# Strassen's scheme for the down projections of both MLPs, with spilled operand quarters

## The chip, the cores and the metric

The kernel runs on one core of one Trainium2 chip. The metric is the device time in microseconds (us) of one execution. TensorE (PE in the profile) multiplies matrices, VectorE (DVE) and ScalarE (ACT) work elementwise and read PSUM, GpSimd (POOL) works elementwise in SBUF, and all DMAs of this kernel are issued from SyncE's queue (SP).

## What is computed

Two layers over 1024 prompt tokens and 32 sample tokens, of width 1024. Layer 0 has a Mamba-2 mixer, layer 1 stick-breaking attention. After each mixer stands the same MLP, and it is all that matters here:

```python
def sq_relu_mlp(h, w_up, w_down):
    return jnp.square(jax.nn.relu(h @ w_up)) @ w_down

y_p = y_p + sq_relu_mlp(rms_norm(y_p, norm_mlp[i]), mlp_up[i], mlp_down[i])
y_s = y_s + sq_relu_mlp(rms_norm(y_s, norm_mlp[i]), mlp_up[i], mlp_down[i])
```

`w_up` is 1024 x 4096 and `w_down` 4096 x 1024, all in float32.

## The kernel before

Both token groups are one activation matrix X of T = 1056 columns (tokens), kept transposed as 8 tiles of 128 rows (features). A float32 product is made of three matmuls: each operand is split into a high part (rounded, type fp32r) and a low part (the rest), and high x high, high x low and low x high are accumulated in PSUM. A split is one copy on ACT (the high part) and one subtraction on DVE (the low part).

The MLP runs twice, as "a" after the Mamba mixer and "b" after attention (`mlp`, L918 to L975); "b" is the end of the kernel.

**Up projection** (class `Up`, L646). The hidden layer has 32 tiles f of 128 rows. Tiles 0 and 1 are made plainly (`plain`, L728). The other 30 are made in 15 pairs by Strassen's scheme (Winograd's form): `pair` (L807) takes two output tiles (f and g), four blocks k of the 1024 inputs, each split in two, and two halves of the tokens (HW = 528 columns each). In place of 8 block products there are 7, of 4 x 3 x 2 = 24 matmuls each, 264 columns wide (`product`, L795, matmuls at L803). The sums of operands on the side of X are made once (`mix12`, `mix4`, `mix3`); those on the side of the weights are made for each pair by `wprep` (L753), whose seven pieces (load, two pieces of sums on POOL and DVE, four splits) are placed as side work between the products of the pair before. The products' results are combined on DVE (L841 to L860), squared on ACT (L834), and spilled to DRAM: tensor `v_d` holds 32 tiles of 128 x 1056, stored in halves at L835. Four PSUM buffers of two banks each rotate.

**Down projection** (L967 to L974). It is plain. In 8 blocks b of four f-tiles each, `mids` (L904) loads the four spilled tiles (L899) and splits them (ACT L900, DVE L901); `down_block` (L625) then goes through the 8 output tiles d, four f-tiles x 3 terms x 3 column groups of 352 (GW) for each, 36 matmuls at L145, and `accum` (L612) adds the PSUM result to X[d] on DVE (L620). Weights come two output tiles at a time (512 KB) through `load_w` (L115: load L117, splits L123 and L124). So a down projection is 8 x 8 x 36 = 2304 matmuls. The X tiles were parked in DRAM (`x_s`) while the up projection used their place, and `reload` (L958) brings them back around the last pair.

The last block of "a" calls `done(d)` after each output tile: X[d] is stored and enters the norm of the attention layer (splits at L185 and L186), and the first projection of attention (L1433) follows. The last block of "b" goes group by group (`gstep`, L164) and stores the output (L1442 to L1446).

**What sets the order.** The program lists the work of all engines in one order; the framework's scheduler then gives each engine its queue, in which an instruction may stand earlier than in the program if its data and buffers are free by then. On the chip each queue runs in order, and an instruction that waits holds up those behind it. SBUF tiles with the same tag share a buffer: a new tile waits until the old one's readers are done.

Of the kernel before, what the change touches and what calls it, by code (L numbers as in the profile page):

```python
# [20 lines left out]
NG = 3  # L21
# [25 lines left out]
NC_COLS = C_HALF + 4  # L47

# [29 lines left out]
def hybrid_step(ctx: ExitStack, tc: tile.TileContext, xt, cst, cbf, w_in, w_dt, w_out, w_up0, w_dn0, w_qkv, w_o,  # L78
# [23 lines left out]
    xg = [None] * KD  # L102

# [23 lines left out]
    def gemm(src, xs, pp, evac, name, f0=0, w=None, tag="g", gmajor=False, mid=None, step=4,  # L127
             grp=GRP):

        box = {}  # L130
        nk = len(xs)

# [4 lines left out]
        def kstep(k):  # L137
            if k == 0:
                start()
# [3 lines left out]
            for i, (a, b) in enumerate(((wh, xh), (wh, xl), (wl, xh))):  # L143
                for g in range(NG):
                    te.matmul(box["ps"][g][:, :GW], a[:, c:c + 128], b[:, GRP[g]],  # L145
                              start=(k == 0 and i == 0), stop=(k == nk - 1 and i == 2))
            if k == nk - 1:
# [23 lines left out]
        return [lambda k=k: kstep(k) for k in range(nk)]  # L171
# [474 lines left out]
    class Up:  # L646
# [5 lines left out]
        def __init__(self, mp, name, gain_col, w, order):  # L652
            self.mp, self.name, self.gain, self.w, self.order = mp, name, gain_col, w, order
            self.v_d = dp.tile([32, 128, T], F32, name=f"v_d{name}", tag=f"v_d{name}")
# [3 lines left out]
            self.prepared = {}  # L658

# [93 lines left out]
        def wprep(self, p):  # L753
# [18 lines left out]
            def sums2():  # L772
# [3 lines left out]
                gp.tensor_tensor(S4, part(r0, 1), part(S, 0), op=ALU.subtract)  # L776

            def split(key):
                raw = w[key]
                if key == "S4":  # L780
                    hi, lo = (self.mp.tile([128, 512], F32R, name=f"w{n}3_{nm}", tag=f"w{n}4", bufs=1) for n in "hl")
                    sc.activation(hi, raw, AF.Copy)
                    ve.tensor_tensor(lo, raw, hi.bitcast(F32), op=ALU.subtract)
                else:
                    hi, lo = split_w(raw, f"{nm}_{key}")
# [8 lines left out]

        def product(self, ps, p, j, ks, first):  # L795

            (wh, wl), c0 = self.prepared[p][j]
            for k in ks:
                c = c0 + 128 * k
                xh, xl = self.ops[j, k]  # L800
                for i, (a, b) in enumerate(((wh, xh), (wh, xl), (wl, xh))):
                    for g in range(2):
                        te.matmul(ps[:, g, :QW], a[:, c:c + 128], b[:, QW * g:QW * g + QW],  # L803
                                  start=(first and k == 0 and i == 0), stop=(k == 3 and i == 2),
                                  skip_group_check=not first)

        def pair(self, p, side):  # L807
# [15 lines left out]
            def two(t):  # L823
                return t[:, :, :QW]

            def sp(x):
                return x.rearrange("p (g n) -> p g n", g=2)

            def out(n, h, e):
# [5 lines left out]
                dma(self.v_d[2 * p + (n == "g")][:, HW * h:HW * h + HW], c)  # L835
# [38 lines left out]
            then()  # L874
            self.product(A, p, 2, K, False)
# [4 lines left out]
            then()  # L880
            B = psum()
            self.product(B, p, 3, K, True)
            p7(B)
            p5(C)
            then()
# [5 lines left out]
            p3(C)  # L891
            while side:
# [11 lines left out]
        def mids(self, b):  # L904

            xs = []
            kind = "xl" if b == 6 else "m" if b % 2 == 0 or b == 7 else "xh"
            for i in range(4):
                h, l = (f"{kind}{2 * i + n}" for n in range(2))
                xs.append(self.parts(self.v_d[4 * b + i], (h, l), f"m{self.name}{b}{i}"))  # L910
            return xs

        def project(self, tail):

            for p in range(1, 16):
                self.pair(p, self.wprep(p + 1) if p < 15 else [lambda: None] * 3 + tail)

    def mlp(X, src, w_last, gain_col, w_up, w_dn, mp, pp, close_pp, stp, name, order, last=None, each=None):  # L918
# [9 lines left out]
        prep = up.wprep(1)  # L928
# [622 lines left out]
```

## Time and profile before

| | us |
|---|---|
| median of 3 runs | 3080.03 (3076.19 to 3080.2) |
| profiled execution | 3083.55 |
| its span, first to last instruction | 3081.8 |
| up projection a, pairs 1 to 15, from | 998.73 |
| down projection a, from | 1305.61 |
| projection that follows, from | 1674.95 |
| up projection b, pairs 1 to 15, from | 2401.25 |
| down projection b, from | 2709.01 |

The starts are those of the chain of work that ended last. The granted TensorE clock is 0.993 over the span. In the profile, `ps_ua` and `ps_da` are the PSUM tiles of the up and the down projection of "a", `ps_ub` and `ps_db` those of "b"; `y_ma`, `yh_ma` and `yo_ma` are a spilled tile, its high and its low part; `ws`, `wh` and `wl` are weights, raw, high and low. A row of a group reads: line, engine, operation, output <- inputs, shapes, count | busy us, mean ns of one | idle us of the engine before them, and what ended it.

### The profile page before, as it was taken

How to read it: one execution, taken by the hardware profiler on the slowest of the kernel's cores; microseconds unless marked ns; L12 is line 12 of the kernel's file. 1: busy time of each engine (PE TensorE's matmuls, PEld its weight loads, DVE VectorE, ACT ScalarE, POOL GpSimd, SP SyncE). 2: the span in 40 equal slices, each digit the busy share in tenths (PEclk: the TensorE clock that was granted, in tenths of full speed). 3: DMA queues.
4: the chain of work that ended last, by engine and by line, in shares of the span. 5: the costliest groups of instructions: out<-in, count | busy, mean ns of one | idle time of the engine just before them, and what ended most of it. 6: DMA issues, size and time to landing. Idle time of an engine off the chain costs nothing.

```text
span 3081.8 us, 52128 instructions
## 1 busy us (share of the span) xinstructions
PE 3020.6 (98%) x21438; PEld 2881.1 (93%) x21438; DVE 1963.1 (64%) x2858; ACT 1168.0 (38%) x1959; POOL 750.0 (24%) x591
## 2 busy tenths in 40 slices
PE   9999999999999999999999999999999999999999
PEld 7899888898999999999999888888889999999999
DVE  7877788776748655644534677677668755554443
ACT  4433333334224333311203466666664433321210
POOL 2666656665100111000002133233230111100000
PEclk9999999999999999999999999999999999999999
DMA  4323333333522433543312322222234323352311
GB/s 134 72 74 79 71 78 84 78 83 93 185 90 92 136 112 102 168 132 105 117 44 85 113 78 71 70 70 71 84 108 141 122 99 112 128 183 84 119 62 71
DMA packets 142631, 308.01 MB, mean 100 GB/s; under 512 B 18380, under 2 KB 67768, under 8 KB 142392
## 3 DMA queue, kind: packets, MB, share of 16 engines
q1 hardware_dynamic: 142392, 304.67, 32.4%
q8 instruction: 169, 2.77, 0.4%
q14 instruction: 70, 0.57, 0.1%
HBM read 220.25 MB, written 75.98 MB: 96 GB/s over the span
## 4 chain that ended last, share of the span: by engine, by line
PE 80%; DVE 13%; issue 3%; ACT 2%; DMA 2%; POOL 1%; SPq 0%; DVEq 0%; ACTq 0%; POOLq 0%
PE ps_da L145 12%; PE ps_db L145 10%; PE ps_ua L803 9%; PE ps_ub L803 9%; PE ps_i L164 9%; PE ps_q L164 3%; PE ps_o L164 3%; PE ps_k L164 2%; PE o L1234 2%; PE wt L1218 2%; PE ps_v L164 2%; PE ps_o L145 2%; PE ps_lb L145 1%; PE ps_db L164 1%; PE ps_la L145 1%
## 5 line engine op out<-in xcount | busy, mean ns | idle before, releaser
L164 PE MATMUL ps_i<-xh_n,wh_i 128*128 128x352 f32 x1056 | 359.3, 340 | 0.0
L164 PE MATMUL ps_i<-xh_n,wl_i 128*128 128x352 f32 x1056 | 343.8, 326 | 0.0
L164 PE MATMUL ps_i<-xl_n,wh_i 128*128 128x352 f32 x1056 | 343.7, 325 | 0.0
L1183 POOL TENSOR_TENSOR b<-b,p 128x255 f32<-128x255 f32 (+7 forms) x128 | 165.3, 1292 | 378.6 <-DVE p L1181 236.4
L1181 DVE TENSOR_TENSOR_SCAN p<-p 128x255 f32<-128x255 f32 (+7 forms) x128 | 192.2, 1502 | 91.7 <-ACT p L1179 90.6
L164 PEld LDWEIGHTS ps_i<-xh_n,wh_i 128*128 128x128 f32 x1056 | 201.8, 191 | 13.5 <-issue 11.6
L620 DVE TENSOR_TENSOR X_b<-X_b,ps_db 128x352 f32<-128x352 f32 x192 | 89.9, 517 | 180.9 <-PE ps_db L145 150.5
L164 PEld LDWEIGHTS ps_i<-xl_n,wh_i 128*128 128x128 f32 x1056 | 203.0, 192 | 0.0
L164 PEld LDWEIGHTS ps_i<-xh_n,wl_i 128*128 128x128 f32 x1056 | 201.3, 191 | 0.0
L620 DVE TENSOR_TENSOR X_a<-X_a,ps_da 128x352 f32<-128x352 f32 x192 | 88.5, 516 | 168.9 <-PE ps_da L145 168.9
L145 PE MATMUL ps_da<-yh_ma,wl_da 128*128 128x352 f32 x768 | 164.8, 323 | 0.0
L145 PE MATMUL ps_da<-yh_ma,wh_da 128*128 128x352 f32 x768 | 164.7, 323 | 0.0
L145 PE MATMUL ps_da<-yo_ma,wh_da 128*128 128x352 f32 x768 | 164.7, 323 | 0.0
L448 ACT ACTIVATE L<-L,naT 128x128 f32<-128x128 f32 (+1 forms) x288 | 89.7, 382 | 166.9 <-POOL L L445 166.9
L145 PE MATMUL ps_db<-yh_mb,wl_db 128*128 128x352 f32 x672 | 144.2, 323 | 0.0
L145 PE MATMUL ps_db<-yh_mb,wh_db 128*128 128x352 f32 x672 | 144.1, 323 | 0.0
L145 PE MATMUL ps_db<-yo_mb,wh_db 128*128 128x352 f32 x672 | 144.1, 323 | 0.0
L145 PEld LDWEIGHTS ps_da<-yh_ma,wl_da 128*128 128x128 f32 x768 | 130.4, 188 | 0.0
L145 PEld LDWEIGHTS ps_da<-yh_ma,wh_da 128*128 128x128 f32 x768 | 130.3, 188 | 0.0
L145 PEld LDWEIGHTS ps_da<-yo_ma,wh_da 128*128 128x128 f32 x768 | 130.3, 188 | 0.0
L1179 ACT ACTIVATE p<-z,qn_q 128x384 f32<-128x384 f32 (+4 forms) x192 | 104.5, 579 | 60.2 <-PE z L1210 29.4
L124 POOL TENSOR_TENSOR wl_i<-ws_i,wh_i 128x1024 fp32r<-128x1024 f32 x44 | 106.5, 2420 | 70.4 <-ACT wh_i L123 70.3
(764 smaller groups left out, 8419.4 us busy)
## 6 DMA issues: line engine op xcount, KB each, us to landing
ws_i<-in_w_in SPq DMA_DIRECT2D x48, 512.0 KB
y_ma<-v_da SPq DMA_DIRECT2D x32, 528.0 KB
y_mb<-v_db SPq DMA_DIRECT2D x32, 528.0 KB
ab<-acs_d SPq DMA_DIRECT2D x64, 256.0 KB
ws_da<-in_w_dn SPq DMA_DIRECT2D x32, 512.0 KB
ws_db<-in_w_dn SPq DMA_DIRECT2D x32, 512.0 KB
ws_a<-in_w_up SPq DMA_DIRECT2D x30, 512.0 KB
ws_b<-in_w_up SPq DMA_DIRECT2D x30, 512.0 KB
```

The lines of the kernel that those rows point to most:

```text
L124: eng[0].tensor_tensor(lo, st, hi.bitcast(F32), op=ALU.subtract)
L145: te.matmul(box["ps"][g][:, :GW], a[:, c:c + 128], b[:, GRP[g]], start=(k == 0 and i == 0), stop=(k == nk - 1 and i == 2))
L164: te.matmul(box["ps"][:, :n], a[:, c:c + 128], b[:, grp[g]], start=(k == 0 and i == 0), stop=(k == nk - 1 and i == 2))
L448: sc.activation(L[0:w, h, :w], L[0:w, h, :w], AF.Exp, bias=naT[0:w, c, 4 * g + h:4 * g + h + 1])
L620: ve.tensor_tensor(X[d][:, GRP[g]], X[d][:, GRP[g]], ps, op=ALU.add)
L803: te.matmul(ps[:, g, :QW], a[:, c:c + 128], b[:, QW * g:QW * g + QW], start=(first and k == 0 and i == 0), stop=(k == 3 and i == 2), skip_ ...
L1179: sc.activation(t[0:np_, c:c + w], ps[0:np_, :w], AF.Sigmoid, scale=sn[0:np_, f])
L1181: ve.tensor_tensor_scan(p[0:np_, 1:W][:, ::-1], p[0:np_, 1:W][:, ::-1], p[0:np_, 1:W][:, ::-1], 1.0, op0=ALU.mult, op1=ALU.bypass)
L1183: gp.tensor_tensor(b[0:np_, 0:W - 1], b[0:np_, 0:W - 1], p[0:np_, 1:W], op=ALU.mult)
L1218: te.transpose(ps[:, c, :], self.b[:, 128 * (c0 + c):128 * (c0 + c) + 128], ident)
L1234: te.matmul(o[r, :128], V[:, c, r], u.wt[c // 4 * 4][:, c % 4, :], start=(c == 0), stop=(c == i))
```

## The change

The down projection uses the same seven-product scheme, for both MLPs. Its 2 x 2 blocks are: two output tiles d (a "pair", four of them), the two f-tiles of one f-pair k (16 of them), and two halves of the tokens.

- Up projection: for each f-pair, `mix` makes four sums of the halves of f and g on DVE, and seven quarters of 128 x 528 (the operands of the seven products) are spilled to `q_d` in place of four to `v_d`. The second half of f is no longer spilled itself. f-pair 0 (from `plain`) is mixed during pair 1. In pair 15, product 3 is moved ahead.
- Down projection: 19 steps in place of 8 blocks. Four f-pairs are resident, as seven split operands each, in the tiles that held the operands of the up projection. A step takes one output pair and all resident f-pairs that it lacks (`STEPS`: two, three and four at the start, mostly four, then three, two and one at the end), and sums them in PSUM. While a step runs, `refill` loads, splits and so replaces one f-pair (7 quarters), each operand right after the product that used it last; `wprep`, now with n f-pairs wide, makes the next step's weights (`w_dn` is laid out anew on the host).
- PSUM: three accumulators U, W, V of two banks in a step, and a fourth buffer from which the next step's U starts. Seven additions of 528 columns to X per step, on DVE; U is read out after each of its four products and then added onto further.
- X tiles return in another order of tags; `done` and the output's stores follow the order in which output pairs end (6, 7, then 0, 1, then 2, 3, then 4, 5), and the next projection takes its inputs in that order (`ks`).

The core of the diff:

```diff
+QPOS = (4, 1, 3, 5, 0, 2, 6)
+ORDER = (0, 2, 1, 4, 3, 6, 5)
+
+STEPS = [(s % 4, ks) for s, ks in enumerate(
+    [range(0, 2), range(0, 3), range(0, 4), range(0, 4), range(2, 5), range(3, 6), range(4, 7)] +
+    [range(max(s - 3, 4), min(s + 1, 16)) for s in range(7, 19)])]
...
+        def mix(self, k, f, g, ta, tb):
+
+            (f0, f1), (g0, g1), (t1, t2), (t3, t4) = ([x[:, HW * h:HW * h + HW] for h in range(2)] for x in (f, g, ta, tb))
+            ve.tensor_tensor(t1, f1, f0, op=ALU.subtract)
+            ve.tensor_tensor(t2, g1, t1, op=ALU.subtract)
+            self.spill(k, 4, ta)
+            ve.tensor_tensor(t3, g1, f1, op=ALU.subtract)
+            ve.tensor_tensor(t4, g0, t2, op=ALU.subtract)
+            self.spill(k, 3, tb)
...
             self.product(C, p, 6, K, False)
             p3(C)
+            self.mix(p, *(box[n] for n in ("f", "g", "t1", "t2")))
...
+        def refill(self, k):
+
+            box = {}
+
+            def f(j):
+                n = ORDER.index(j)
+                if n % 2 == 0:
+                    box["y"] = self.mp.tile([128, T], F32, name=f"y_{self.name}{k}{j}", bufs=2 if n < 4 else 1,
+                                            tag=("sq", "sq", "acc", "u0")[n // 2])
+                    for i, jj in enumerate(ORDER[n:n + 2]):
+                        dma(box["y"][:, HW * i:HW * i + HW], self.q_d[k, QPOS.index(jj)])
+                t = self.ttile(DTAGS[k % 4][n], f"d{j}_{self.name}{k}")
+                self.split(j, ("d", k), box["y"][:, HW * (n % 2):HW * (n % 2) + HW], t[:, 0:HW], t[:, HW:T])
+
+            return [lambda j=j: f(j) for j in ORDER]
...
+        def step(self, s, X, side, each):
...
+            ps = {n: self.psum.tile([128, 2, 512], F32, name=f"ps_d{self.name}{s}{n}", tag=f"d{r[n]}") for n in "UWV"}
+            self.roles = {"U": r["F"], "V": r["W"], "W": r["V"], "F": r["U"]}
+            K = [("d", k) for k in ks]
+            for n, (j, c, first, d, h, end) in enumerate((
+                    (0, "U", True, d1, 0, False), (2, "W", True, d1, 0, True), (1, "U", False, d1, 1, False),
+                    (4, "V", True, d2, 1, False), (3, "U", False, d2, 1, True), (6, "V", False, d1, 1, True),
+                    (5, "U", False, d2, 0, True))):
+                self.product(ps[c], f"d{s}", j, K, first)
+                x = self.sp(X[d][:, HW * h:HW * h + HW])
+                ve.tensor_tensor(x, x, self.two(ps[c]), op=ALU.add)
+                if end:
+                    each(d, h)
+                for t in side:
+                    if n < len(t) and t[n]:
+                        t[n]()
...
-            self.pair(p, self.wprep(p + 1) if p < 15 else [lambda: None] * 3 + tail)
+                prep = self.up_weights(p + 1) if p < 15 else tail
...
-            up.project([lambda: box.update(xs=up.mids(0)), first, lambda: reload((0, 1, 3, 5))])
-        reload((2, 4, 6, 7))
+            up.project([lambda: (dw[0](), reload((0, 1))), dw[1], lambda: (run(r0[:3]), dw[2]()),
+                        lambda: (run(r0[3:6]), dw[3]()), lambda: (run(r0[6:] + r1[:3]), dw[4]()),
+                        lambda: (run(r1[3:5]), dw[5](), reload((2, 3))), lambda: (dw[6](), run(r1[5:]))])
+        reload(range(4, KD))
...
-        for b in range(8):
-            end = b == 7
-            blk = down_block(w_dn[b], box["xs"], X, pp, f"d{name}{b}", done if end else None, gmajor=bool(each) and end,
-                             each=each if end else None, first=box.pop("w", None))
+        refills = {0: r2, 1: up.refill(3), **{s: up.refill(k) for s, k in ((3, 4), (4, 5), (5, 6), (6, 7))},
+                   **{s: up.refill(s + 1) for s in range(7, 15)}}
...
+            for s, (pair, _) in enumerate(STEPS):
...
+                side = [refills.get(s, [])]
+                if s + 1 < len(STEPS):
+                    side.append(up.down_weights(s + 1))
+                up.step(s, X, side, finished)
```

More of the change, by code (lines that the diff above doesn't have):

```diff
@@ L102, in hybrid_step @@
     xg = [None] * KD
+    xtags = [(f"xh{d}", f"xl{d}") for d in range(KD)]
     rota = {"ws": [0, 1], "wh": [0, 1, 2], "wl": [0, 1, 2]}
@@ L803, in product, with two, sp @@
                         te.matmul(ps[:, g, :QW], a[:, c:c + 128], b[:, QW * g:QW * g + QW],
-                                  start=(first and k == 0 and i == 0), stop=(k == 3 and i == 2),
+                                  start=(first and n == 0 and i == 0), stop=(n == len(ks) - 1 and i == 2),
                                   skip_group_check=not first)
+        def two(self, t):
+            return t[:, :, :QW]
+        def sp(self, x):
+            return x.rearrange("p (g n) -> p g n", g=2)
         def pair(self, p, side):
@@ L874, in pair @@
             then()
+            if p == 15:
+                B = psum()
+                self.product(B, p, 3, K, True)
+                p7(B)
+                then()
             self.product(A, p, 2, K, False)
@@ L879, in pair @@
             self.product(C, p, 4, K, True)
[L880 to L885, printed above, removed]
+            if p == 15:
+                p5(C)
+                then()
+            else:
+                then()
+                B = psum()
+                self.product(B, p, 3, K, True)
+                p7(B)
+                p5(C)
+                then()
             B = psum()
@@ L950, in mlp, with reload @@
         close_pp()
+        up.w_dn = w_dn
+        hold = [f"h{order[d]}" for d in (0, 1, 3, 5, 2, 4, 6, 7)]
+        r0, r1, r2 = (up.refill(k) for k in range(3))
+        dw = up.down_weights(0)
+        def reload(ds):
+            for d in ds:
+                X[d] = hx.tile([128, T], F32, name=f"X_{name}{d}", tag=hold[d])
+                dma(X[d], up.x_s[d])
         with ExitStack() as pu:
             up.psum = pu.enter_context(tc.tile_pool(name=f"pu{name}", bufs=4, space=PSUM, reuse_waits="tile"))
-            box = {}
@@ new lines, in mlp, with finished @@
+        reload(range(4, KD))
+        done = last(mp) if last else None
+        final = {pair: s for s, (pair, _) in enumerate(STEPS)}
+        refills = {0: r2, 1: up.refill(3), **{s: up.refill(k) for s, k in ((3, 4), (4, 5), (5, 6), (6, 7))},
+                   **{s: up.refill(s + 1) for s in range(7, 15)}}
+        with ExitStack() as pd:
+            up.psum = pd.enter_context(tc.tile_pool(name=f"pd{name}", bufs=1, space=PSUM, reuse_waits="tile"))
+            up.roles = {"U": 0, "V": 2, "W": 3, "F": 1}
+            for s, (pair, _) in enumerate(STEPS):
+                ended = []
+                def finished(d, h):
+                    if final[d // 2] != s:
+                        return
+                    if each:
+                        each(d, h)
+                    ended.append(d)
+                    if done and ended.count(d) == 2:
+                        done(d)
+                side = [refills.get(s, [])]
+                if s + 1 < len(STEPS):
+                    side.append(up.down_weights(s + 1))
+                up.step(s, X, side, finished)
```

116 lines of the change are left out of this document (65 added, 51 removed).

## The prediction

> **What bounds the kernel now.** I read the page's busy table first, then the chain in order of time, then the busy table by stage, then the groups of the engines that the change loads.
>
> ```profile
> span 3081.8 us, 52128 instructions
> PE 3020.6 (98%) x21438; PEld 2881.1 (93%) x21438; DVE 1963.1 (64%) x2858; ACT 1168.0 (38%) x1959; POOL 750.0 (24%) x591
> PE 80%; DVE 13%; issue 3%; ACT 2%; DMA 2%; POOL 1%; SPq 0%; DVEq 0%; ACTq 0%; POOLq 0%
> ```
>
> TensorE (PE) carries 80% of the chain that ended last. The next rows are pieces of that chain (start, length, what):
>
> ```profile
> 998.73 289.13 PE ps_ua L803 x2382
> 1292.08 6.50 DMA y_ma<-v_da
> 1302.45 3.16 PE ps_ua L803 x24
> 1305.61 369.34 PE ps_da L145 x2304
> 1674.95 11.62 PE ps_k L145 x72
> 2401.25 285.40 PE ps_ub L803 x2352
> 2709.01 323.22 PE ps_db L145 x2016
> 3032.23 46.09 PE ps_db L164 x288
> ```
>
> The down projection of the first MLP is one unbroken run of 2304 matmuls, 352 columns wide: 369.34/2304 = 160.3 ns each. The second takes 323.22 + 46.09 = 369.31 us. The up projection, already in Strassen's form, uses 264 columns: 289.13/2382 = 121.4 and 285.40/2352 = 121.3 ns; I use 121.35. So time per matmul follows the columns almost exactly (121.35/160.3 = 0.757, 264/352 = 0.75). One piece on the chain is no matmul: a DMA at 1292, between up and down. By stage (us, then busy time of PE, its weight loads, DVE, ACT, POOL; granted clock, DMA share, GB/s):
>
> ```profile
> 998.70:1284.00 285.30, 285.30 (x2353) 285.30 (x2352) 170.50 (x223) 97.57 (x132) 40.57 (x28) 1.00 0.34 113
> 1284.00:1305.60 21.60, 20.80 (x171) 20.59 (x170) 13.99 (x17) 10.68 (x13) 0.00 (x0) 1.00 0.86 291
> 1305.60:1328.00 22.40, 22.40 (x142) 22.40 (x141) 12.11 (x18) 6.61 (x8) 0.00 (x0) 1.00 0.88 307
> 1328.00:1674.90 346.90, 346.90 (x2166) 346.90 (x2165) 156.04 (x242) 72.92 (x68) 15.13 (x6) 1.00 0.28 90
> 1301.50:1320.00 18.50, 17.70 (x117) 17.55 (x116) 11.42 (x16) 7.26 (x9) 0.00 (x0) 1.00 0.96 341
> PE ps_ua L803 <- DVE g_a L851: 0.8, 1, 0.8
> PE ps_ub L803 <- DVE g_b L851: 1.7, 1, 1.7
> ```
>
> Both projections keep PE full at granted clock 1.00 with VectorE (DVE) at 60% and 45%. The seam between them is different: DMA at 0.86 to 0.96 of its engines, 341 GB/s at best, and PE waits 0.8 us there in the first MLP, 1.7 us in the second (last two rows).
>
> **The matmuls (the gain).** New count per MLP: 4 output pairs x 16 f-pairs x 7 products x 3 (high/low terms) x 2 column groups = 2688, all 264 wide, same operand forms as the up projection. 2688 x 0.12135 = 326.2 us against 369.3: 43.1 us less per MLP, 86.3 us for both (738.65 - 652.4).
>
> [...]
>
> **DVE in a step of the new loop.** The rows that price it:
>
> ```profile
> L859 DVE TENSOR_TENSOR f_b<-ps_ub,t_b 128x528 f32<-128x528 f32 x14 | 9.9, 707 | 2.1 <-PE ps_ub L803 2.1
> L699 DVE TENSOR_TENSOR xl_ub<-u_b,xh_ub 128x528 fp32r<-128x528 f32 x4 | 2.6, 706 | 0.0
> L783 DVE TENSOR_TENSOR wl_b<-wS_b,wh_b 128x512 fp32r<-128x512 f32 x15 | 10.2, 682 | 0.0
> L124 DVE TENSOR_TENSOR wl_da<-ws_da,wh_da 128x1024 fp32r<-128x1024 f32 x32 | 39.0, 1219 | 0.2 <-ACT wh_da L123 0.2
> L770 DVE TENSOR_TENSOR ws_b<-ws_b 128x512 f32<-128x512 f32 x14 | 9.7, 693 | 34.2 <-POOL wS_b L769 34.2
> L123 ACT ACTIVATE wh_da<-ws_da 128x1024 fp32r<-128x1024 f32 x32 | 33.9, 1059 | 204.5 <-PE ps_da L145 193.5 <-DVE yo_ma L901 6.6 <-PE ps_ua L803 2.3
> L834 ACT ACTIVATE g_a<-g_a x28: 625/628/648, 1017.8 to 1284.6; 128x528 f32<-128x528 f32 x28
> L769 POOL TENSOR_TENSOR wS_a<-ws_a,ws_a x14: 1287/1295/4735, 1006.7 to 1266.8; 128x512 f32<-128x512 f32 x14
> ```
>
> A step that takes four f-pairs: 168 matmuls, 20.4 us of PE. DVE: 7 additions from PSUM into X at 0.707 (4.9), 7 low parts of refilled operands at 0.706 (4.9), weights 3 x 1.219 + 0.682 + 2 x 0.693 = 5.7; together 15.5 us. ScalarE (ACT): 7 x 0.628 + 3 x 1.059 + 0.6 = 8.2. POOL: 2 x 1.295 = 2.6. All under 20.4, so hidden. A step of three (steps 1, 4, 5, 6, 16; 15.3 us of PE): weights shrink to three quarters, about 4.4, so 14.2 us, and 15.5 where the step after it takes four. That is 93 to 101% of PE's time, on a queue that runs in order: I take 1 us of PE waiting per MLP, bounds 0 (instructions start 0.62 us apart back to back, rows below) and 5 (1 us in each). The additions have cover: U is added to X after each of its four products, and PE writes U again only one product later, 2.9 us in a step of four, against 0.7 us of addition. If the DVE queue ran later than that, PE would wait for all that exceeds it.
>
> In the up projection each pair gains 4 subtractions (4 x 0.706 = 2.8 us of DVE) and 3 quarters more of spill. DVE goes from 170.50/285.30 = 60% to about 74%, DMA from 113 GB/s to some 153 (0.81 MB more per 20.4 us). The subtractions stand behind the pair's last read of PSUM, and the next one is due two products (5.8 us) later: that hides them, and I cost them at nothing; without that cover a pair would lose at most these 2.8 us.
>
> **The seam.** Most of the loss should lie here. Rows for it:
>
> ```profile
> 1280.90 0.70 DVE L833 SCALAR_TENSOR_TENSOR g_a<-g_a,rstd 128x528 f32<-128x528 f32 x1
> 1281.52 0.70 DVE L855 TENSOR_TENSOR g_a<-ps_ua,t_a 128x528 f32<-128x528 f32 x1
> 1282.21 1.23 DVE L124 TENSOR_TENSOR wl_a_raw<-ws_a,wh_a_raw 128x1024 fp32r<-128x1024 f32 x1
> 1283.35 0.70 DVE L833 SCALAR_TENSOR_TENSOR g_a<-g_a,rstd 128x528 f32<-128x528 f32 x1
> 1010.75 1.58 SPq L899 DMA_DIRECT2D y_ma<-v_da  x2
> 1290.32 2.08 SPq L899 DMA_DIRECT2D y_ma<-v_da  x2
> v_da<-f_a SPq DMA_DIRECT2D x30, 264.0 KB
> y_ma<-v_da SPq DMA_DIRECT2D x32, 528.0 KB
> ws_da<-in_w_dn SPq DMA_DIRECT2D x32, 512.0 KB
> ```
>
> Back to back, a 528-wide instruction starts 0.62 us after the one before, a 1024-wide one takes 1.14. The program places the loads of the first spilled tiles in the last pair, but the first two left at 1010.75, as soon as data and buffers were there; so the loads of f-pair 0 (four free buffers) will be early too. The rest is not. DMA: from about 16 us before the end of pair 15 to the start of step 2 (16 + 25.5 us; steps 0 and 1 are 84 + 126 matmuls), the queue moves 11 quarters of spill and 21 of refill for f-pairs 1 to 3 (32 x 0.27 MB), eight X tiles (8 x 0.54) and the weights of steps 1 and 2 (0.79 + 1.05): 14.8 MB. At 341 GB/s that is 43.4 us against 41.5. DVE: between the end of pair 15 and step 2, some 32 instructions of 528 (2 for the last quarter of pair 15, 4 mixing, 14 additions, 12 low parts) at 0.63 are 20.2 us, the weights of step 1 about 4.0 and the first half of step 2's 3.5: 27.7 us against 25.5. Both are 2 us over. As a refill load must wait for the split that frees its buffer, they don't overlap perfectly: I take 5 us per MLP, bounds 0 and 15 (one third of the 43.4). PE's present 0.8 + 1.7 us fall into these, so the seams cost 2 x 5 - 2.5 = 7.5 net.
>
> **The ends.**
>
> ```profile
> 3078.35 0.52 DVE L620 TENSOR_TENSOR X_b<-X_b,ps_db 128x352 f32<-128x352 f32 x1 [1.40 <-PE ps_db L164]
> L186 DVE SCALAR_TENSOR_TENSOR xl_n<-X_a,cs,xh_n 128x1056 fp32r<-128x1056 f32 x7 | 9.2, 1319 | 5.3 <-ACT xh_n L185 5.0
> ```
>
> The last step takes one f-pair: 42 matmuls, 0.73 us a product. The addition (0.707) no longer hides behind one product, and seven of them in a row need 7 x 0.707 = 4.9 of its 5.1 us, with a turn between PE and DVE at each write of U: 1 us of waiting, and 0.2 for a wider last addition (0.707 for 0.52). In the second MLP I take 1.5. In the first, two low parts of the norm (1.319 each) stand in the same DVE queue, and the next projection wants the PSUM banks of U: 2.5. It starts with d = 6 and 7, done four steps before, and reaches d = 4 and 5 six eighths of 11.62 us later, so those splits are hidden. Together 4, bounds 1 and 8.
>
> **Sum.** Span 3081.8 and the profiled execution's 3083.55 us; the median of the runs is 3080.03, 3.5 lower. 3083.55 - 86.3 + 2 x 1 + 7.5 + 4 = 3010.75; less 3.5: 3007 us.
>
> **Rivals.**
> (1) The seam is worse: SP's queue, in order, holds refill and weight loads behind X tiles that wait for pair 15's spills. For: the DMA on the chain at 1292. Against: X from f-pair 2 on is wanted only 25 us later. At the upper bound, 15 us a seam, it gives 3007 + 20 = 3027.
> (2) DVE's in-order queue becomes the bound in every step, and the kernel is slower. Each of the 11 low parts per step stands behind a copy on ACT, which stands behind a load; while DVE waits, additions behind it wait, and PE for them. The present loop does show such waits:
>
> ```profile
> L901 DVE TENSOR_TENSOR yo_ma<-y_ma,yh_ma 128x1056 fp32r<-128x1056 f32 x32 | 40.2, 1258 | 33.2 <-ACT yh_ma L900 33.1
> ```
>
> 33.2/32 = 1.04 us before each. With a wait w, the 14 steps with refills take 213 + 154w us (9 + 4 of them at 15.5 or 14.2 plus 11w, step 0 likewise), the others 73: equal to 369.3 at w = 0.54, where this decides. At 1.04 the loop takes 446 us, 76.5 more per MLP: 3080 + 153 = 3233. Against: DVE had nothing else queued in those waits, and before the weights' low parts, which have the same shape of dependency, the wait is 0.2 us over 32 (the L124 row).
> (3) A matmul costs the same at 264 as at 352 columns, as it would if weight loads set the pace: 2688 x 160.3 ns = 430.9 us, 61.6 more per MLP, 3203. Against: the 121.35 ns of the up projection, which loads as many weights per matmul. [...]
>
> **How the numbers follow.** Measurement tells about 0.2% (6 us) from no change. Chances: the forecast 0.75 (2992 to 3022), (1) 0.15, (2) 0.06 (of it 0.02 near w = 0.54, within 0.2%), (3) 0.01, and 0.03 for a result below 2992, since nothing in the sum gains beyond the matmuls. Faster 0.93, same 0.02, slower 0.05. Range: all unknown costs at their lower bounds give 3080 - 86.3 - 2.5 + 1 = 2992; at their upper, 3080 - 86.3 - 2.5 + 30 + 10 + 8 = 3039.
>
> **What would show it.** Right: the down groups count 2688 matmuls each at the up projection's 283 ns duration, in a run of 326 to 330 us; PE waits for DVE or DMA gather in the 45 us around the seam and the last 10 us of each down loop; DVE 75% busy between. Wrong: waits of PE on the additions to X spread over all steps (2); one gap of 10 us or more after pair 15 with DMA at 0.9 (1); a mean spacing well above 121 ns without waits (3).

## The result, and the profile after

| | before | after |
|---|---|---|
| median of 4 runs, us | 3078.21 (3076.19 to 3080.2) | 3095.03 (3091.33 to 3097.83) |
| profiled span, us | 3081.8 | 3096.1 |
| mean granted TensorE clock | 0.993 | 0.987 |

After/before is 1.0054 (95% interval 1.0037 to 1.0071): slower by 0.5%, where 3007 us was forecast. The forecast was wrong by 88 us, and in sign. The page of the profile after, its span, busy table and chain:

```profile
span 3096.1 us, 55134 instructions
PE 2962.8 (96%) x22206; PEld 2809.7 (91%) x22206; DVE 2272.8 (73%) x3192; ACT 1292.1 (42%) x2207; POOL 851.6 (28%) x667
PE 64%; DVE 20%; DMA 5%; issue 5%; ACT 3%; POOL 2%; SPq 0%; DVEq 0%; POOLq 0%; ACTq 0%
```

PE has less work, as forecast, but only 64% of the chain is PE now (80% before): DVE, DMA and issue have taken its place. The busy table by stage, first for most of up projection "a", then for steps 4 to 14 of its down projection (columns as in the prediction):

```profile
1000.00:1285.00 285.00, 281.98 (x2322) 281.56 (x2321) 213.41 (x274) 95.89 (x130) 42.23 (x28) 1.00 0.45 154
1399.00:1629.70 230.70, 214.47 (x1725) 211.66 (x1724) 165.92 (x217) 84.17 (x118) 30.56 (x22) 0.99 0.42 129
```

In the up projection the load is as forecast (DVE 75%, 154 GB/s) and PE misses 3 us. In the down projection PE idles 16.2 of 230.7 us, although no other engine is near full (DVE 72%): that is waiting, not work. The waits of PE and of DVE in steps 7 to 13 of "a" (engine, line, waited for: us in total, times, longest):

```profile
PE ps_da8U L857 <- DVE X_a L1018: 2.1, 1, 2.1
PE ps_da12U L857 <- DVE X_a L1018: 1.9, 1, 1.9
PE ps_da10U L857 <- DVE X_a L1018: 1.8, 1, 1.8
...
DVE ws_ad L819 <- POOL wS_ad L818: 20.1, 7, 3.3
DVE d_a L719 <- ACT d_a L718: 9.4, 15, 0.7
```

Each step has one wait of PE for an addition to X (L1018), and one wait of DVE, 20.1/7 = 2.9 us, in a sum of weights (L819) for POOL's sum (L818). How the two hang together is seen in step 8, on SP, POOL, DVE and PE (start, length, engine, line; at the end, the idle time before it and what ended it):

```profile
1473.78 0.55 SPq L810 DMA_DIRECT2D ws_ad<-in_w_dn  x1
...
1478.62 1.29 POOL L818 TENSOR_TENSOR wS_ad<-ws_ad,ws_ad 128x512 f32<-128x512 f32 x1 [17.81 <-DMA ws_ad<-in_w_dn]
1481.99 1.61 POOL L825 TENSOR_TENSOR wS_ad<-ws_ad,wS_ad 128x512 f32<-128x512 f32 x1 [2.08 <-DVE wS_ad L823]
...
1479.93 0.69 DVE L819 TENSOR_TENSOR ws_ad<-ws_ad 128x512 f32<-128x512 f32 x1 [3.27 <-POOL wS_ad L818]
1480.54 0.69 DVE L1018 TENSOR_TENSOR X_a<-X_a,ps_da8W 128x528 f32<-128x528 f32 x1
1481.16 0.68 DVE L823 TENSOR_TENSOR wS_ad<-ws_ad,ws_ad 128x512 f32<-128x512 f32 x1
1481.76 0.70 DVE L719 TENSOR_TENSOR d_a<-y_a,d_a 128x528 fp32r<-128x528 f32 x1
1482.38 2.30 DVE L836 TENSOR_TENSOR wl_ad_raw<-ws_ad,wh_ad_raw 128x1024 fp32r<-128x1024 f32 x1
1484.61 0.69 DVE L1018 TENSOR_TENSOR X_a<-X_a,ps_da8U 128x528 f32<-128x528 f32 x1
...
1485.35 0.75 PE L857 MATMUL ps_da8U<-d_a,wh_ad_S 128*128 128x264 f32 x4 [2.09 <-DVE X_a L1018]
```

Read it from the top. There are two buffers for raw weights. The second load for step 9 leaves SP at 1473.78, when the split that reads that buffer is over; POOL subtracts when it has landed (1478.62); DVE's sum waits 3.27 us for POOL and holds up what is queued behind it: the addition of W, three more operations, and the addition of U at 1484.61, for which PE stands still 2.09 us. One of the operations between, the low part of a weight, took 2.30 us where the same form takes 1.23 elsewhere; POOL works beside it from 1481.99.

The seam shows something else. The same table, before in the first row, after in the others:

```profile
1310.00:1325.00 15.00, 15.00 (x95) 15.00 (x95) 7.71 (x13) 3.77 (x4) 0.00 (x0) 1.00 0.94 321
```

```profile
1315.00:1320.00 5.00, 3.08 (x24) 2.87 (x24) 4.58 (x8) 1.93 (x3) 0.00 (x0) 1.00 0.89 287
1320.00:1325.00 5.00, 1.84 (x6) 1.53 (x7) 2.38 (x5) 0.84 (x1) 1.03 (x2) 0.52 0.95 343
1325.00:1330.00 5.00, 5.00 (x24) 5.00 (x24) 3.36 (x4) 1.13 (x2) 0.97 (x1) 0.50 0.91 325
1330.00:1335.00 5.00, 5.00 (x42) 5.00 (x41) 3.47 (x5) 3.46 (x6) 0.00 (x0) 0.96 1.04 388
```

PE stood still for 3.88 us from 1318.1, for a weight of step 1:

```profile
1321.95 1.25 PE L857 MATMUL ps_da1U<-d_a,wh_ad_raw 128*128 128x264 f32 x4 [3.88 <-ACT wh_ad_raw L835]
```

The granted clock fell to 0.50 in the course of this wait: from 1325 to 1330 PE was busy throughout and made 24 matmuls where 42 fit. In the clock record of this trace the fall stands at 1320.2, 2.1 us into the wait, and the clock stayed at half for 10.2 us. PE was busy for 7.3 of these, which at half the clock lost 3.6 us: so that wait was paid nearly twice. In that time PE had one more gap, of 1.21 us; whether this delayed the return isn't shown.

### The profile page after: what moved, and what is told of

Same layout as the page of the kernel before. It is cut to its first block, busy times and chain, and to the rows that moved or that the text cites. A ratio compares the mean times of both kernels' runs of the same rounds, so it can differ in the third digit from the quotient of the medians.

```text
span 3096.1 us, 55134 instructions
## 1 busy us (share of the span) xinstructions
PE 2962.8 (96%) x22206; PEld 2809.7 (91%) x22206; DVE 2272.8 (73%) x3192; ACT 1292.1 (42%) x2207; POOL 851.6 (28%) x667
## 4 chain that ended last, share of the span: by engine, by line
PE 64%; DVE 20%; DMA 5%; issue 5%; ACT 3%; POOL 2%; SPq 0%; DVEq 0%; POOLq 0%; ACTq 0%
PE ps_i L181 9%; PE ps_ub L857 9%; PE ps_ua L857 8%; PE ps_q L181 3%; PE ps_o L181 3%; PE ps_k L181 2%; PE o L1356 2%; PE wt L1340 2%; PE ps_v L181 2%; PE ps_o L162 2%; PE ps_lb L162 1%; PE ps_p L181 1%; DVE p L1303 1%; DMA ws_ad<-in_w_dn 1%; PE ps_la L162 1%
## 5 line engine op out<-in xcount | busy, mean ns | idle before, releaser
L818 POOL TENSOR_TENSOR wS_a<-ws_a,ws_a 128x512 f32<-128x512 f32 x15 | 24.9, 1661 | 387.0 <-DMA ws_a<-in_w_up 372.8
L140 POOL TENSOR_TENSOR wl_i<-ws_i,wh_i 128x1024 fp32r<-128x1024 f32 x44 | 105.4, 2395 | 73.7 <-ACT wh_i L139 73.5
L463 POOL TENSOR_TENSOR L<-ab,cs 128x512 f32<-128x512 f32 (+1 forms) x72 | 103.1, 1433 | 52.9 <-PE pb L498 43.4
L718 ACT ACTIVATE d_b<-y_b 128x528 fp32r<-128x528 f32 x112 | 70.8, 640 | 110.6 <-DMA y_b<-q_db 16.5
L718 ACT ACTIVATE d_a<-y_a 128x528 fp32r<-128x528 f32 x112 | 70.7, 640 | 107.1 <-DMA y_a<-q_da 13.8
L1340 PE MATMUL wt<-cs,b 128*128 128x128 f32 x576 | 90.4, 281 | 14.8 <-DVE wts L1345 12.3
L1301 ACT ACTIVATE b<-z,qn_q 128x384 f32<-128x384 f32 (+4 forms) x192 | 104.3, 584 | 0.0
L818 POOL TENSOR_TENSOR wS_bd<-ws_bd,ws_bd 128x512 f32<-128x512 f32 (+3 forms) x19 | 21.9, 1153 | 296.4 <-DMA ws_bd<-in_w_dn 272.1
L818 POOL TENSOR_TENSOR wS_b<-ws_b,ws_b 128x512 f32<-128x512 f32 x15 | 24.0, 1600 | 284.6 <-DMA ws_b<-in_w_up 254.6
L818 POOL TENSOR_TENSOR wS_ad<-ws_ad,ws_ad 128x512 f32<-128x512 f32 (+3 forms) x19 | 23.3, 1225 | 275.6 <-DMA ws_ad<-in_w_dn 255.8
L719 DVE TENSOR_TENSOR d_b<-y_b,d_b 128x528 fp32r<-128x528 f32 x112 | 82.0, 742 | 21.6 <-ACT d_b L718 20.9
L719 DVE TENSOR_TENSOR d_a<-y_a,d_a 128x528 fp32r<-128x528 f32 x112 | 81.0, 735 | 18.4 <-ACT d_a L718 17.5
```

The lines of the kernel that those rows point to most:

```text
L140: eng[0].tensor_tensor(lo, st, hi.bitcast(F32), op=ALU.subtract)
L463: gp.tensor_tensor(L[0:w, :, :w], ab[0:w, :, :w], cs[0:w, None, C_MASK:C_MASK + w].to_broadcast([w, 4, w]), op=ALU.add)
L718: sc.activation(hi, x, AF.Copy)
L719: ve.tensor_tensor(lo, x, hi.bitcast(F32), op=ALU.subtract)
L818: gp.tensor_tensor(part(S, 1), part(r0, 0), part(r1, 0), op=ALU.subtract)
L1301: sc.activation(t[0:np_, c:c + w], ps[0:np_, :w], AF.Sigmoid, scale=sn[0:np_, f])
```

## Where the time went

A step's length is taken from its first matmul on U to that of the next; "over" is what goes beyond 121.35 ns per matmul (66.3 us for steps 0 to 3, 244.6 for 4 to 16, 15.3 for 17 and 18, in each MLP). Both MLPs together, against the profiled execution before; the two columns on the right are the second and the twelfth experiment below:

| us | forecast | after | sums behind additions | all once more |
|---|---|---|---|---|
| matmuls | -86.3 | -86.3 | -86.3 | -86.3 |
| all ahead of the first down loop | 0 | +5.1 | +8.1 | +6.3 |
| steps 0 to 3, over | +10 | +37.4 | +20.6 | +12.6 |
| steps 4 to 16, over | +2 | +43.5 | +3.0 | +1.3 |
| steps 17 and 18, over (less 3.5 at the end of before) | +4 | +15.3 | +16.2 | +10.1 |
| from the first down loop to the second | 0 | -0.7 | -1.4 | +7.2 |
| sum (the forecast less 2.5 for waits of before) | -73 | +14 | -40 | -49 |

The spans differ by +14.3, -39.8 and -48.9.

## The experiments

Theory A: DVE's in-order queue. A sum of weights that waits for a late load stands ahead of additions to X that are due, and PE waits for those. Rival B: POOL's sums beside them stretch DVE's operations with two SBUF inputs (2.30 us for 1.23 in step 8), and PE waits for that. Rival C: the bytes at the seam.

Each measurement below is the median of four runs in us, then its ratio to the kernel before, run beside it, with the 95% interval.

**1. A third buffer for raw weights.** The down loop's raw weights rotate over three tiles (the third is one that lies idle there), so that a load needn't wait for the last split.

```diff
-                    w[f"raw{i}"] = wtile("ws", F32, f"{nm}_{i}")
+                    slot = raws.pop(0) if raws else None
+                    if slot is not None:
+                        raws.append(slot)
+                    w[f"raw{i}"] = (wtile("ws", F32, f"{nm}_{i}") if slot is None else rstd[:, 0:1024] if slot == 2 else
+                                    wp.tile([128, 1024], F32, name=f"ws_{nm}_{i}", tag=f"ws{slot}"))
```

> Edit: in the down loop the raw weights rotate over three buffers (the two of before and the idle tile rstd), so the loads for the next step no longer wait for the last split of this one. Theory A (the additions to X stand in VectorE's in-order queue behind a weight sum that waits for a late load; PE waits 1.7 us for them in each step of four): the wait of VectorE for POOL before L819 goes, steps 7 to 14 take 20.5 to 21 us in place of 22.4, the kernel gains 20 to 30 us (about 3068). Rival B (VectorE is short of time because POOL's two sums block its instructions with two SBUF inputs): POOL works as much as before, steps stay at 22 us, 3090 to 3095.

Measured: 3050.58 us, 0.9907 (0.9892 to 0.9922). Steps 7 to 15 took 20.4 us each in both MLPs (22.0 to 24.2 for 7 to 14 after the change). In step 7 of this run:

```profile
1462.55 0.69 DVE L823 TENSOR_TENSOR ws_ad<-ws_ad 128x512 f32<-128x512 f32 x1 [1.19 <-POOL wS_ad L822]
1463.16 0.70 DVE L1023 TENSOR_TENSOR X_a<-X_a,ps_da7V 128x528 f32<-128x528 f32 x1
...
1466.22 1.98 DVE L840 TENSOR_TENSOR wl_ad_raw<-rstd,wh_ad_raw 128x1024 fp32r<-128x1024 f32 x1
```

(Edits shift the line numbers of some runs: L823 and L840 here are L819 and L836 above.) With the load no longer late the sum waits 1.19 us, less than POOL's own 1.29, and PE no longer waits in these steps. The stretched operation is still there (1.98 us): a stretch of that size alone didn't make PE wait here.

**2. The weight sums behind the additions.** Only the order on DVE: both sums are placed after the third product, and side work is issued behind the addition of the same product.

```diff
-                ve.tensor_tensor(x, x, self.two(ps[c]), op=ALU.add)
+                added = ve.tensor_tensor(x, x, self.two(ps[c]), op=ALU.add)
...
-                        t[n]()
+                        with tc.issue_after(added.ins):
+                            t[n]()
...
-                    side.append(up.down_weights(s + 1))
+                    load, s1, s2, *rest = up.down_weights(s + 1)
+                    side.append([load, None, lambda s1=s1, s2=s2: (s1(), s2()), *rest])
```

> Edit: order alone. The weight sums of the next step are queued behind the third addition to X, and each piece of side work behind the addition that it follows in the program; loads, buffers and engines stay. Theory A: the load is as late as before, but nothing that PE wants stands behind it; steps 7 to 14 take 20.5 to 21 us, gain 20 to 30 us, as with a third buffer. Rival B: VectorE does the same work under the same contention, 22 us, no gain. If the later sums only move the wait to the splits (raw 0 is due at the next step), less than half of the gain shows.

Measured: 3043.8 us, 0.9882 (0.9868 to 0.9897), 51 us less than the changed kernel. A steady step of it by engine, then DVE in step 9:

```profile
1454.50:1474.90 20.40, 20.40 (x170) 20.40 (x169) 14.90 (x20) 7.99 (x11) 2.58 (x2) 1.00 0.47 146
```

```profile
1480.91 0.70 DVE L1018 TENSOR_TENSOR X_a<-X_a,ps_da9W 128x528 f32<-128x528 f32 x1 [1.51 <-PE ps_da9W L857]
1481.53 0.70 DVE L719 TENSOR_TENSOR d_a<-y_a,d_a 128x528 fp32r<-128x528 f32 x1
1483.83 0.70 DVE L1018 TENSOR_TENSOR X_a<-X_a,ps_da9U 128x528 f32<-128x528 f32 x1 [1.60 <-PE ps_da9U L857]
1484.45 0.70 DVE L719 TENSOR_TENSOR d_a<-y_a,d_a 128x528 fp32r<-128x528 f32 x1
1485.07 0.69 DVE L819 TENSOR_TENSOR ws_ad<-ws_ad 128x512 f32<-128x512 f32 x1
1485.79 0.69 DVE L823 TENSOR_TENSOR wS_ad<-ws_ad,ws_ad 128x512 f32<-128x512 f32 x1
```

The additions now wait for PE, not PE for them; the sum waits for nothing. PE is busy for the whole step, with the forecast's work on the others (DVE 14.9 us for 15.5, ACT 8.0 for 8.2, POOL 2.6 for 2.6). This shows A for the steady state, by order alone. The stretch of B is gone from these rows too, but as a consequence.

**3. Both sums on VectorE** in the down loop, so that DVE needn't wait for POOL.

```diff
-                gp.tensor_tensor(part(S, 1), part(r0, 0), part(r1, 0), op=ALU.subtract)
+                (ve if nm.find('d') >= 0 else gp).tensor_tensor(part(S, 1), part(r0, 0), part(r1, 0), op=ALU.subtract)
...
-                gp.tensor_tensor(part(S4, 0), part(r0, 1), part(S, 0), op=ALU.subtract)
+                (ve if nm.find('d') >= 0 else gp).tensor_tensor(part(S4, 0), part(r0, 1), part(S, 0), op=ALU.subtract)
```

> Edit: in the down loop both POOL sums of a step's weights are done on VectorE (2 x 0.69 us more there, POOL idle). Theory A: the load is still late, only POOL's 1.3 us leave the wait, so PE's wait per step shrinks from 1.7 to about 0.4 and steps of four take about 21.2; gain 10 to 20 us. Rival B: the 2.3 us splits beside POOL go back to 1.2; steps at 20.5, gain 25 to 30 us.

Measured: 3044.11 us, 0.9888 (0.9871 to 0.9904); steps 7 to 15 at 20.4 us. From its step 9:

```profile
1481.12 0.69 DVE L818 TENSOR_TENSOR wS_ad<-ws_ad,ws_ad 128x512 f32<-128x512 f32 x1 [1.48 <-DMA ws_ad<-in_w_dn]
1481.73 0.70 DVE L1018 TENSOR_TENSOR X_a<-X_a,ps_da9W 128x528 f32<-128x528 f32 x1
```

DVE still waits for the load, 1.48 us, and PE for nothing: without POOL's 1.29 us and without the stretch, the 2.9 us of cover that the forecast names are enough. So load, POOL and stretch together exceeded the cover, by 1.3 to 2.1 us per step, and each of three cures takes enough away. The stretch by itself is not enough for a wait of PE (experiment 1), and neither is the late load by itself (this one). For the shares the rows of step 8 allow an estimate: without the stretch of 1.07 us (2.30 less 1.23) PE would have waited about 1 us there in place of 2.09, and without DVE's wait of 3.27 us not at all.

All three gained more than expected, 44 to 51 us where 10 to 30 was said. The expectations went by the steps of four f-pairs, 7 to 14; the late sums cost in the steps ahead of them as well (experiment 2 took 40.5 us off steps 4 to 16 and 16.8 off steps 0 to 3).

**4. X tiles 4 to 7 reloaded in steps 1 and 2** instead of ahead of step 0 (C).

```diff
-        reload(range(4, KD))
...
+                if s in (1, 2):
+                    reload((2 * s + 2, 2 * s + 3))
```

> Edit: X tiles 4 to 7 are reloaded at steps 1 and 2 and no longer ahead of step 0's refills in SP's queue. Theory C (at the seam SP's queue holds refill and weight loads behind X loads that wait for the last pair's spills): steps 0 to 2 together shrink from 66.5 us in the first MLP and 59.3 in the second by 5 to 10 us each, gain 10 to 20 us. Rival D (the seam is bound by the DMA bytes alone, about 300 GB/s): the same bytes are only moved, gain under 4 us.

Measured: 3094.11 us, 1.0042 (1.0027 to 1.0057), no gain. Steps 0 to 2 of "a" shrank from 66.5 to 56.2 us, those of "b" stayed (59.4, 59.7), and "a" started its loop 4.4 us later.

All that follow contain the edit of the second experiment (3043.8 us, 0.9882), whose losses lie ahead of the loop, in steps 0 to 3 and at the end.

**5. All together:** experiments 1, 2 and 4, and 6 and 8 below.

> The weight sums behind the additions, the third raw buffer, X tiles 4 to 7 reloaded in steps 1 and 2, the first pair's four mixing operations dealt out one at a time, and the norm's accumulation at the end of the first MLP on VectorE, all together. Theory: what is left of the loss lies in separate places (the seam into the down loop, the first pair of the up loop, the tail of the first MLP), at each a wait of PE of 2 to 3 us and behind it some microseconds at half the granted clock, so the gains add: 3044 less 8 to 15 (seam) less 6 to 9 (first pair) less 5 to 10 (tail) = 3010 to 3025 us. Rival, a wait removed in one place is only taken up by the next queue: 3030 us or more.

Measured: 3043.18 us, 0.9875 (0.9859 to 0.9892). The rival holds: no addition of gains.

**6. The next norm's additions on VectorE,** in the last steps of "a".

```diff
-                (ve if self.n == KD - 1 else gp).tensor_tensor(self.acc, self.acc, s, op=ALU.add)
+                (ve if self.n == KD - 1 or self.name == 'n2' else gp).tensor_tensor(self.acc, self.acc, s, op=ALU.add)
```

> As the kernel with the sums behind the additions (3043.8 us), with one edit: the next norm's additions in the last two steps of the first MLP (128x1056, both inputs in SBUF) go from POOL to VectorE. What is computed is the same. Theory that POOL's additions hold VectorE up when both work from SBUF: the splits of the next layer's operands (3.10 us beside POOL, 1.32 alone) come back to 1.32, which is worth more than the 1.32 us that each addition then costs VectorE; PE's waits of 8.4 us and the half clock behind them shrink: 5 to 10 us less, 3034 to 3039 us. Rival, VectorE simply has too much to do there: no gain or a loss, 3043 to 3050 us.

Measured: 3043.4 us, 0.9876 (0.9860 to 0.9892). The low part that the norm needs, beside POOL in experiment 2, and its followers on DVE in this run:

```profile
1637.58 2.60 POOL L265 TENSOR_TENSOR acc_n<-acc_n,sq_n 128x1056 f32<-128x1056 f32 x1 [0.60 <-ACT sq_n L261]
1638.40 2.89 DVE L204 SCALAR_TENSOR_TENSOR xl_n<-X_a,cs,xh_n 128x1056 fp32r<-128x1056 f32 x1
```

```profile
1645.44 1.31 DVE L204 SCALAR_TENSOR_TENSOR xl_n<-X_a,cs,xh_n 128x1056 fp32r<-128x1056 f32 x1
1646.67 1.25 DVE L265 TENSOR_TENSOR acc_n<-acc_n,sq_n 128x1056 f32<-128x1056 f32 x1
```

2.89 + 0 against 1.31 + 1.25 us of DVE: a small gain. Smaller operations lost more here. Two low parts of the last weights beside POOL's additions in experiment 2, then the same two in this run:

```profile
1648.85 5.20 POOL L265 TENSOR_TENSOR acc_n<-acc_n,sq_n 128x1056 f32<-128x1056 f32 x2 [4.65 <-ACT sq_n L261]
1649.12 2.66 DVE L836 TENSOR_TENSOR wl_ad_raw<-ws_ad,wh_ad_raw 128x256 fp32r<-128x256 f32 x1
1651.70 2.50 DVE L836 TENSOR_TENSOR wl_ad<-wS_ad,wh_ad 128x128 fp32r<-128x128 f32 x1
```

```profile
1647.84 0.41 DVE L836 TENSOR_TENSOR wl_ad_raw<-ws_ad,wh_ad_raw 128x256 fp32r<-128x256 f32 x1
1648.79 0.28 DVE L836 TENSOR_TENSOR wl_ad<-wS_ad,wh_ad 128x128 fp32r<-128x128 f32 x1
```

With one more low part (2.36 us for 0.68), four operations of DVE are stretched by 7.7 us in all in the last two steps of experiment 2, so B counts in the tail. Steps 17 and 18 of "a" fell from 29.6 to 24.8 us, but from the first down loop to the second took 2.8 us more. What fills the tail is DVE; here is experiment 2 in its last two steps of "a":

```profile
1633.40:1643.00 9.60, 7.16 (x54) 6.54 (x54) 9.60 (x10) 3.83 (x5) 6.60 (x3) 1.00 0.27 106
1643.00:1653.00 10.00, 6.68 (x51) 6.05 (x49) 8.35 (x10) 6.17 (x8) 4.66 (x3) 0.96 0.55 168
1653.00:1663.00 10.00, 6.02 (x24) 5.43 (x25) 9.35 (x12) 2.92 (x3) 1.05 (x1) 0.50 0.23 92
```

DVE is busy 27.3 of 29.6 us (7.7 of them the stretch), PE has work for 15.3; behind PE's gaps the clock is at 0.50 for the last 10.

**7. The new order and X later:** the edit of experiment 4 on top of 2.

> As the kernel with the sums behind the additions (3043.8 us), and X tiles 4 to 7 reloaded at steps 1 and 2 instead of ahead of step 0 (2.2 MB less ahead of step 1). Theory that the bytes queued at the seam set its waits: steps 0 to 2 (53.2 and 59.0 us against 45.9 of PE work) come down to 46 to 50 each, the granted clock stays at 1.00 there, 3029 to 3036 us. Rival, the wait only moves to step 2 or ahead of step 0, as it did without the new order: 3041 to 3046 us.

Measured: 3045.46 us, 0.9882 (0.9867 to 0.9897): steps 0 to 2 at 54.1 and 58.4 us (53.2 and 59.0 without). Nothing gained; the wait moves.

**8. The first pair's mixing in pieces.** The four operations that mix f-pair 0 (all in one piece of pair 1's side work before) go behind four products, one each (`mix0` now returns them as a list).

```diff
-                    prep.insert(3, self.mix0)
+                    prep = [lambda fs=fs: run(fs) for fs in zip(prep, self.mix0() + [lambda: None] * 3)]
```

> As the kernel with the sums behind the additions (3043.8 us), with one edit: in the first pair of the up loop the four mixing operations of the plainly computed pair are issued one behind each of four products instead of four together. Theory: four operations of 0.7 us in a row ahead of the combination of g hold PE's accumulator for 2.2 + 0.9 us per MLP, and the clock is halved for some microseconds behind it; both go: 6 to 9 us less over both MLPs, 3035 to 3038 us. Rival, VectorE's work of the whole pair is too long and the wait moves to a later product: 3042 to 3045 us.

Measured: 3045.29 us, 0.9883 (0.9868 to 0.9898); PE waits the same 2.2 + 0.8 us there. POOL and DVE in that pair (L835 and L853 are L818 and L836 above):

```profile
1009.50 5.47 POOL L835 TENSOR_TENSOR wS_a<-ws_a,ws_a 128x512 f32<-128x512 f32 x1 [30.02 <-DMA ws_a<-in_w_up]
...
1018.07 2.31 DVE L853 TENSOR_TENSOR wl_a_raw<-ws_a,wh_a_raw 128x1024 fp32r<-128x1024 f32 x1
```

DVE has a gap of only 0.58 us between 1002 and 1026, which fits the rival, too much work in the pair. Beside DVE's operations POOL's sum takes 5.47 us here (1.29 elsewhere), and beside POOL's later one a low part of DVE takes 2.31.

**9. X tiles 4 to 7 loaded twice** ahead of step 0: C by addition, on top of 2.

```diff
+        for d in range(4, KD):
+            dma(X[d], up.x_s[d])
```

> As the kernel with the sums behind the additions (3043.8 us), and X tiles 4 to 7 are loaded twice ahead of step 0 (2.2 MB more in each seam, nothing else changed). Theory that bytes set the waits of the seam: 2.2 MB at the seam's 300 to 400 GB/s are 5 to 7 us per MLP, and more with the clock halved behind a longer wait: 3054 to 3062 us. Rival, the seam's waits are those of single transfers standing behind waiting issues in SP's queue, and of VectorE's work there: within 3 us, 3041 to 3047 us.

Measured: 3052.86 us, 0.9908 (0.9893 to 0.9923), 9 us more than without, between the two. Steps 0 to 3 of "a" grew by 6.3 us, of "b" by 1.2. So the added loads do cost in "a"; fewer (7) gained nothing. The edit puts four more loads into SP's queue ahead of the refills as well, so bytes and order are not told apart.

**10. The spills of pair 15 late:** its five spills and its mixing come behind step 0, with the edits of 2 and 4.

```diff
-                if (n, h) != ("f", 1):
+                if (n, h) != ("f", 1) and p < 15:
...
+            def late():
+                for n, h in (("f", 0), ("g", 0), ("g", 1)):
+                    self.spill(p, 0 if n == "f" else 6 if h else 2, half(n, h))
+                self.mix(p, *(box[n] for n in ("f", "g", "t1", "t2")))
...
                 up.step(s, X, side, finished)
+                if s == 0:
+                    up.late()
```

> As the kernel with the new order and X later (3045.5 us), and the last up pair's five spills and its four mixing operations come behind step 0 of the down loop instead of inside the pair. Theory that SP's queue holds the last refill loads behind spills that wait for values still being computed (SP waited 3 to 4 us on the spill of g, PE then 2.7 to 3.3 us for the last refilled operand of step 0, and half the granted clock followed for 10 us and more in the second MLP): steps 0 to 2 of the second MLP come down from 58 to 47 to 50 us, of the first from 54 to 48 to 51: 3031 to 3040 us. Rival, the splits of 14 operands on ACT and VectorE take as long as step 0 in any case, or the later spills hold up the reload of X: 3042 to 3050 us.

Measured: 3040.62 us, 0.9874 (0.9858 to 0.9891). Steps 0 to 3 came to 70.7 and 77.4 us (73.6 and 79.5 in experiment 2, 74.6 and 78.8 in 7): a part of the rival (1) of the prediction seems to be there, worth 1 to 4 us per MLP, less than expected. The time of the whole kernel doesn't show it, as the interval overlaps those of 2 and 7.

**11. And the weights ahead of the refills** in steps 0 to 2, on top of 10.

```diff
+                if s < 3:
+                    side.reverse()
```

> As the run with the last pair's spills late, and in steps 0 to 2 the next step's weight loads and splits are issued ahead of the refills instead of behind them. Theory that PE's wait of 3.0 to 3.7 us in step 1 of the first MLP on the high part of a weight comes from the load standing behind refill loads in SP's queue: that wait goes, another 3 to 6 us less with the clock, 3027 to 3036 us. Rival, the refills then come late for step 2 or 3: no change or up to 5 us more.

Measured: 3042.68 us, 0.9878 (0.9863 to 0.9892); steps 0 to 3 at 71.6 and 77.1 us. No change.

**12. All once more:** 11 with 1, 3 and 6.

> As the run before, with the third raw buffer, the weight sums of the down loop on VectorE and the next norm's additions on VectorE added: each part by itself left the steady state at PE's own time. Theory that what is left stands in the seam and the tail alone: these parts bring no more than 5 us on top, 3022 to 3036 us. Rival, VectorE is by now the bound of seam and tail, and its added work costs 3 to 8 us: 3032 to 3044 us.

Measured: 3030.84 us, 0.9839 (0.9822 to 0.9855): the best version, 1.6% under before and 64 us under the changed kernel. It is 12 us under 11, where no more than 5 was expected. Against 11, steps 17 and 18 of "a" lost 6.2 us (29.6 to 23.5), steps 0 to 3 of "b" 2.5 (to 74.5); which of the three parts does it isn't told apart. The seam of "b" in experiment 2, PE's first long wait and then the table behind it:

```profile
2703.52 0.81 PE L857 MATMUL ps_db0V<-d_b,wh_bd_raw 128*128 128x264 f32 x2 [2.70 <-ACT d_b L718]
```

```profile
2703.00:2717.00 14.00, 11.29 (x46) 10.37 (x47) 12.21 (x20) 4.50 (x8) 2.80 (x2) 0.52 0.97 341
```

And the same in 12:

```profile
2699.04 0.51 PE L861 MATMUL ps_db0V<-d_b,wh_bd_raw 128*128 128x264 f32 x2 [2.53 <-ACT d_b L718]
```

```profile
2700.00:2717.00 17.00, 14.77 (x114) 13.92 (x114) 17.00 (x29) 11.31 (x18) 0.00 (x0) 1.00 0.94 295
```

In 2, the wait of 2.70 us is followed by 14 us at clock 0.52, in which PE is busy for 11.29 us: 0.48 x 11.29 = 5.4 us lost to the clock. In 12 the wait is 2.53 us and the clock stays at 1.00. That may be luck: a wait of 2.53 us in a seam was followed by 3.4 us at half the clock in experiments 3 ("a") and 10 ("b"). PE still has gaps in 12, and DVE is busy in all of the 17 us.

## Why the prediction was wrong

**The matmuls: right.** With the waits away, a step of 168 is 20.4 us, and -86.3 us stands: 20.4/168 = 121.4 ns a matmul. Rival (3), with 160.3 ns, falls with it for the matmuls of this kernel.

**DVE in a step: the step that failed.** "All under 20.4, so hidden" added up busy times, which were right to 4%, and let the queue run on time by assumption. "If the DVE queue ran later than that, PE would wait for all that exceeds it" was the right condition, but its size wasn't worked out. The warning stood in a quoted row: the up loop's sum of weights (L770) waits 34.2/14 = 2.4 us for POOL each time. It cost nothing there; in the down loop an addition with 2.9 us of cover stands behind it, and a load that leaves late for want of a third buffer stands in front. POOL's 2.6 us were "hidden" by the same argument, without the hand-over. Steps 4 to 16: forecast 2, measured 43.5 us. The prediction's sign of failure, "waits of PE on the additions to X spread over all steps", is what the trace shows.

**Rival (2): the right kind, the wrong instruction, and far too small a chance (0.06).** It put the wait in the 11 low parts. Those of the refilled operands (L719, seven a step) wait 9.4 us in seven steps, 0.19 us each on average. The one sum waits 2.9 us per step. The evidence against (2), the 0.2 us in the L124 row, came from weights with one load and no sum.

**The seam and the ends: too low.** Steps 0 to 3 cost 37.4 us for 10 (bound 30). Part is the same late sum (a wait of 6.2 us in step 2 of "a" behind one), as experiment 2 took 16.8 off; part is the clock. Neither bytes (4, 7, 9) nor SP's order (10, 11) settles the rest: fewer bytes gained nothing net, the added loads cost 7.6 us in these steps, the later spills took 4.9 off. The estimate that DVE would be 2 us over in 25.5 may have had the right place: DVE is full in experiment 12, though there it also does POOL's sums. At the ends 15.3 us for 4 (bound 8): two steps of a tail in which, in experiment 2, DVE is busy for 27 us and PE has work for 15. The forecast counted seven additions and two low parts of the norm. In experiment 2 those two steps hold five of the norm (L204), six low parts and two sums of the last weights (L836, L819, L823) and two low parts of the next projection's (L140), with 7.7 us of stretch beside POOL in four of them. The prediction allowed nothing for that stretch.

**Nothing was allowed for the clock.** The mean granted clock fell from 0.993 to 0.987. In the two down loops the clock record has 38 us at half the clock, where the kernel before has none, and PE's busy time lost 14 us in them, of the 96 that steps 0 to 18 cost. A bound of waits that counts each once is too low.

**The up projection: nearly nothing, as forecast,** but for the first pair: 2.2 + 0.8 us of waits per MLP, at the bound of 2.8 for a pair. In "a" this is the greater part of the 5.1 us ahead of the first down loop.

**The stretch between the down loops** has nearly the same work in the changed kernel and all its variants, and took from 1030.8 (experiment 1) to 1041.2 us (12). The clock record accounts for it: it has 6.8 us at half the clock there in experiment 1, 13.1 in 2 and 33.2 in 12, in which PE's busy time lost 3.4, 6.6 and 15.6 us. Less this loss, all thirteen lie at 1025.6 to 1027.8 us. So a difference of some us between two whole kernels can come from the clock in a part that the edit doesn't touch; the lengths of the steps tell more.

**Open:** why the clock falls in one run and not in another behind the same stall, and what share of the seam is DVE's. And the forecast's 3007 us was not reached.

## What to carry to other kernels

Busy time under 100% doesn't by itself hide work on an in-order engine (DVE was at 72% in steps 4 to 14 of "a", and PE idled for 16.2 of 230.7 us): list, for each instruction on which the bottleneck waits, what stands ahead of it in its queue and what that waits for (a load, another engine), and compare the sum with the cover. Where such a wait appeared here, an earlier load, another order or fewer hand-overs were each enough, and another order needs no buffer and moves no work. Count a stall of TensorE for more than its length: with the clock behind it, those of 2.7 to 6.2 us in the seams of the changed kernel and of experiment 2 cost about 1.4 to 3 times their own length.

## What the runs showed of the hardware

- **The clock:** half the granted clock followed some stalls of TensorE, for 3.4 to 13.7 us. In the traces of the changed kernel and its twelve variants all 26 stalls of 2.6 us or more in the projections of the two MLPs were followed by it or fell into it. Shorter stalls were so only at times: the stall of 2.2 us in the first up pair, the same in every one of these traces, in 17 of 26 cases, and those of 1.3 to 2.1 us in steps 7 to 14 of the changed kernel in two of 16 (1.94 us in step 12 of "a", 1.81 us in step 8 of "b", each with 3.4 us at half behind it). So the length alone doesn't decide.
- **DVE beside POOL:** a DVE operation with two SBUF inputs took 2.30 us for 1.23 (step 8 of the changed kernel), 2.89 for 1.31 and 2.50 for 0.28 (the tail of experiment 2, against 6) beside a POOL operation, and POOL's sum took 5.47 for 1.29 beside DVE's (experiment 8). The rows show the stretch in both directions; what in the chip brings it about isn't shown.
